# Reordering one DMA queue: from turns of four loads and four stores to turns of three and three

## The chip, the cores and the metric

The kernel runs on one core of one Trainium2 chip. The metric is the device time of one execution in microseconds (us), median over executions. The profile's span, from the first to the last instruction of one profiled execution, is some 1.8 us shorter than the device time of the same execution. TensorE multiplies, VectorE casts, ScalarE copies and SyncE only issues transfers here; PSUM is the memory in which TensorE leaves its products (`ps` in the code). "y of 5" stands for the y of batch 5.

## The reference

```python
def setup_inputs():
    batch, m, k, n = 16, 512, 768, 1024
    return {
        "x": np.random.randn(batch, k, m).astype(np.float32),
        "y": np.random.randn(batch, k, n).astype(np.float32),
    }

def reference(x, y):
    return np.einsum('bkm,bkn->bmn', x, y).astype(np.float32)
```

These are sixteen independent products. Each batch reads 1.57 MB of x and 3.15 MB of y and writes 2.10 MB.

## The kernel before

Every transfer is issued by SyncE, so all go through one DMA queue, in program order. Batch b passes through these stages:

- `load(b)` brings x and y of b into float32 staging tiles (two of each);
- VectorE casts them to bf16 (two of each) and may do so once TensorE has finished batch b-2;
- TensorE multiplies in two groups, each of which fills one half of PSUM;
- ScalarE copies each half into the output buffer `ob[b % 5]`, once store b-5 has landed, and frees the half of PSUM;
- `store(c)` writes batch c out. Its wait is for TensorE to be done with batch c+1, which implies that c has been copied.

```python
    FIRST = 8
    TURN = 4
    NO = 5
    # ... (cut)
    def store(b):
        if b < B - 2:
            nc.sync.wait_ge(groups, 2 * (b + 2))
        else:
            nc.sync.wait_ge(outs, b - (B - 3))
        nc.sync.dma_start(o_v[b], ob[b % NO][:]).then_inc(so[b % NO], 16)

    def load(b):
        i = b % 2
        if b >= 2:
            nc.sync.wait_ge(cast, nx[b - 2])
        wide_dma("x", xs[i][:], x_v[b], 4, True).then_inc(sx[i], 16)
        if b >= 2:
            nc.sync.wait_ge(cast, nx[b - 2] + parts(b - 2))
        wide_dma("y", ys[i][:], y_v[b], 2, True).then_inc(sy[i], 16)

    for b in range(B):
        load(b)
        if b + 1 >= FIRST and (b + 1 - FIRST) % TURN == 0:
            a = b + 1 - FIRST
            for c in range(a, a + TURN):
                store(c)
    for b in range(B - FIRST + TURN, B - 1):
        store(b)

    nc.sync.wait_ge(outs, 2)
    nc.sync.dma_start(o_v[B - 1, :, :HB], ob[(B - 1) % NO][:, :HB]).then_inc(last, 16)
    # ... (cut: casts on VectorE, `ready` on GpSimd)
    with nc.Fori(0, B // 2, engines=pe):
        with nc.Fori(0, 2, engines=pe) as s:
            nc.tensor.wait_ge(ready, 2).then_inc(ready, -2)
            for mo in range(MT):
                g, m = divmod(mo, HB)
                if m == 0:
                    nc.tensor.wait_ge(room, 1).then_inc(room, -1)
                for kt in range(KT):
                    # ... (cut: wait for the second part of y)
                    for nt in range(NT):
                        mm = nc.tensor.matmul(ps[g][:, m, nt], x_w[:, bass.ds(s, 1), kt, mo],
                            yb[:, bass.ds(s, 1), kt, nt * NF:(nt + 1) * NF],
                            start=(kt == 0), stop=(kt == KT - 1))
                if m == HB - 1:
                    mm.then_inc(groups, 1)
    # ... (cut)
    for b in range(B):
        if b >= NO:
            nc.scalar.wait_ge(so[b % NO], 16 * (b // NO))
        for g in range(2):
            nc.scalar.wait_ge(groups, 2 * b + g + 1)
            cp = nc.scalar.copy(ob[b % NO][:, g * HB:(g + 1) * HB].rearrange("p m (t f) -> p m t f", f=NF),
                                ps[g][:])
            if b < B - 1:
                cp.then_inc(room, 1)
            else:
                cp.then_inc(outs, 1)
    # ... (cut)
    for b in range(B - NO, B - 2):
        nc.sync.wait_ge(so[b % NO], 16 * (b // NO + 1))
    section.close()
    nc.sync.dma_start(o_v[B - 1, :, HB:], ob[(B - 1) % NO][:, HB:])
```

Of the kernel before, what the change touches and what calls it, by code (L numbers as in the profile page):

```python
# [3 lines left out]

# [2 lines left out]

# [8 lines left out]
def kernel(  # L16
# [11 lines left out]
    B, K, M = x.shape  # L28
# [9 lines left out]
    y_v = y.rearrange("b (p ko) n -> b p ko n", ko=KT)  # L38
    o_v = out.rearrange("b (p mo) n -> b p mo n", mo=MT)

    FIRST = 8
    TURN = 4
    NO = 5
    KH = KT // 2

# [25 lines left out]
    def wide_dma(key, dst, src, dram_rows, load):  # L71


        if key not in made:
            made[key] = nc.sync.dma_start(dst, src)
            return made[key]
        pat = mybir.BassSymbolicTensorAccessPattern
        widen = lambda a: a.rearrange("(q r) k m -> q (r k m)", r=dram_rows)
        plain = lambda a: a.rearrange("p k m -> p (k m)")
        s, d = (widen(src), plain(dst)) if load else (plain(src), widen(dst))  # L80
        return nc.sync.add_instruction(_copy.replace(
            made[key].ins, name=nc.get_next_instruction_name(),
            ins=(pat(ap=s.ap, dtype=s.dtype, bass_ap=s, is_dma=False),),
            outs=(pat(ap=d.ap, dtype=d.dtype, bass_ap=d, is_dma=False),),
            sync_info=None, ant_dge_precooked=False))


    def parts(b):
        return 2 if b in (15,) else 1
# [2 lines left out]
    nx = [sum(1 + parts(a) for a in range(b)) + 1 for b in range(B)]  # L92



    def store(b):


# [12 lines that stand above are left out]
            nc.sync.wait_ge(cast, nx[b - 2] + parts(b - 2))  # L111
        wide_dma("y", ys[i][:], y_v[b], 2, True).then_inc(sy[i], 16)

    for b in range(B):
        load(b)
        if b + 1 >= FIRST and (b + 1 - FIRST) % TURN == 0:
            a = b + 1 - FIRST
            for c in range(a, a + TURN):
                store(c)
    for b in range(B - FIRST + TURN, B - 1):  # L120
        store(b)


    nc.sync.wait_ge(outs, 2)
# [100 lines left out]
```

## Time and profile before

| | before |
|---|---|
| device time, median of 3 | 260.67 us (260.51 to 260.77) |
| span of the profiled execution | 258.8 us |
| TensorE / VectorE / ScalarE busy | 69% / 32% / 24% |
| DMA queue busy, mean rate | 98.6%, 421 GB/s |
| waits of ScalarE for a store (output buffer) | 3, in total 61.9 us |

In these profiles a line of a timeline reads: start, duration, engine, source line, operation, output from input, shapes, count. The bracket gives how long the engine had been idle before and what ended that. The prediction shows these lines and works from them. The last row of the table is this line of the waits, with the longest wait at its end:

```profile
ACT ob L178 <- DMA out_dram<-ob: 61.9, 3, 21.7
```

### The profile page before, as it was taken

Reading aid. Unit: us, or ns where it says so; the run is one execution under the profiler, and the core shown is the slowest. Engines: PE = TensorE matmul, PEld = TensorE weight load, DVE = VectorE, ACT = ScalarE, POOL = GpSimd, SP = SyncE. Lnnn points to the kernel's source line nnn. Section 1 sums busy time; section 2 is a strip of 40 time slices with the busy share of each in tenths; the row PEclk is TensorE's granted clock in tenths of the full one; section 3 lists DMA queues with packets and bytes.
Section 4 is the critical chain, followed back from the end, with each engine's and each line's share of the span. In section 5 each row is a group of like instructions: output and inputs, shape, how many; then the busy total and the mean of one; then the engine's idle time right before and its main releaser. Section 6 shows DMA issues by size and latency. Waiting matters only on the chain. (4 is left out here: it accounts for less than half of the span.)

```text
span 258.8 us, 2419 instructions
## 1 busy us (share of the span) xinstructions
PE 178.6 (69%) x768; PEld 88.8 (34%) x768; DVE 82.0 (32%) x33; ACT 60.9 (24%) x33; POOL 0.2 (0%) x4
## 2 busy tenths in 40 slices
PE   0019999999999007996599800999579970199950
PEld 0004555555544003553255400455235530045520
DVE  0271644527255250021643624002345272300000
ACT  1000432243220004234022002224302200413430
POOL 0000000000000000000000000000000000000000
PEclk9999999999999756999799975699979995569995
DMA  6999989898999999999999999999899999999996
GB/s 262 444 479 395 486 365 486 365 486 380 471 403 448 377 420 438 453 458 418 433 433 418 441 387 436 420 463 471 380 486 387 463 395 399 436 433 420 441 415 265
DMA packets 4658, 109.07 MB, mean 421 GB/s; under 512 B 784, under 2 KB 784, under 8 KB 784
## 3 DMA queue, kind: packets, MB, share of 16 engines
q1 hardware_dynamic: 4656, 109.06, 98.6%
q14 instruction: 2, 0.02, 0.0%
HBM read 75.50 MB, written 33.55 MB: 421 GB/s over the span
## 5 line engine op out<-in xcount | busy, mean ns | idle before, releaser
L162 PE MATMUL ps<-yb,xb 128*128 x768 | 178.6, 397 | 70.7 <-PEq L157 70.6
L162 PEld LDWEIGHTS ps<-yb,xb 128*128 x768 | 88.8, 116 | 160.0 <-issue 88.5
L178 ACT COPY ob<-ps 128x2048 f32<-128x2048 f32 x32 | 59.6, 1872 | 188.3 <-PE ps L162 126.4
L140 DVE CAST yb<-ys 128x6144 bf16<-128x6144 f32 (+1 forms) x17 | 53.8, 3171 | 80.1 <-DMA ys<-in_y_dram 80.1
L136 DVE CAST xb<-xs 128x3072 bf16<-128x3072 f32 x16 | 28.2, 1760 | 60.0 <-DMA xs<-in_x_dram 48.8
L178 ACT ACT_TABLE_LOAD x1 | 1.3, 1283 | 2.0 <-issue 2.0
L209 POOL MEMSET const-bfloat16-1.0<- 128x1 bf16 x1 | 0.1, 101 | 0.0
L209 POOL MEMSET const-uint8-127<- 128x1 uint8 x1 | 0.1, 101 | 0.0
L209 POOL MEMSET const-float32-0.0<- 128x1 f32 x1 | 0.1, 98 | 0.2 <-issue 0.2
L209 POOL MEMSET const-float32-1.0<- 128x1 f32 x1 | 0.1, 98 | 0.0
## 6 DMA issues: line engine op xcount, KB each, us to landing
ys<-in_y_dram SPq DMA_DIRECT2D x16, 3072.0 KB, 18.6
out_dram<-ob SPq DMA_DIRECT2D x15, 2048.0 KB, 27.4
xs<-in_x_dram SPq DMA_DIRECT2D x16, 1536.0 KB, 20.1
out_dram<-ob SPq DMA_DIRECT2D x2, 1024.0 KB, 7.9
```

Of the source, the lines that this page charges most:

```text
L136: nc.vector.tensor_copy(xb[:, i], xs[i][:]).then_inc(cast, 1)
L140: nc.vector.tensor_copy(yb[:, i, ks], ys[i][:, ks]).then_inc(cast, 1)
L162: mm = nc.tensor.matmul(ps[g][:, m, nt], x_w[:, bass.ds(s, 1), kt, mo], yb[:, bass.ds(s, 1), kt, nt * NF:(nt + 1) * NF], start=(kt == 0), ...
L178: cp = nc.scalar.copy(ob[b % NO][:, g * HB:(g + 1) * HB].rearrange("p m (t f) -> p m t f", f=NF), ps[g][:])
L209: nc = _bacc.Bacc("TRN2", target_bir_lowering=False, num_devices=1)
```

## The change

The intent is shorter turns. ScalarE, and TensorE behind it, should wait less long for an output buffer, and one store's worth less should be left after the last load. Nothing is added or taken away: SyncE issues the same 49 transfers with the same waits, and only their order differs.

```diff
-    FIRST = 8
-    TURN = 4
+    TURNS = [(7, 3), (3, 3), (3, 3), (3, 7)]
     NO = 5
@@
-    for b in range(B):
-        load(b)
-        if b + 1 >= FIRST and (b + 1 - FIRST) % TURN == 0:
-            a = b + 1 - FIRST
-            for c in range(a, a + TURN):
-                store(c)
-    for b in range(B - FIRST + TURN, B - 1):
-        store(b)
+    loads, stores = iter(range(B)), iter(range(B - 1))
+    for nl, ns in TURNS:
+        for b in islice(loads, nl):
+            load(b)
+        for b in islice(stores, ns):
+            store(b)
```

The last store is issued apart in two halves, so "7 stores last" are six whole ones and two halves; before, there were seven whole ones and two halves.

More of the change, by code (lines that the diff above doesn't have):

```diff
@@ L6 @@
 from contextlib import ExitStack
+from itertools import islice
 import concourse.bass as bass
```

## The prediction

> **What bounds the kernel now.** I read the page from the top. Part 1 gives TensorE 69% of the span, VectorE 32% and ScalarE 24%, so no compute engine is full. Parts 2 and 3 show what is full:
>
> ```profile
> DMA  6999989898999999999999999999899999999996
> ...
> q1 hardware_dynamic: 4656, 109.06, 98.6%
> ...
> HBM read 75.50 MB, written 33.55 MB: 421 GB/s over the span
> ...
> PE 9%; ACT 1%; issue 0%
> ```
>
> The first line is the busy share of the 16 DMA engines in 40 slices: 8 or 9 tenths from the second slice to the last but one. The second gives the queue 98.6% of 16 engines' time. The fourth is the chain of waits, and it misleads: it follows only 10% of the span back from the last ScalarE copy, not the transfers that land after that copy. I set it aside and time the queue itself.
>
> For that I use an idle engine as a clock. VectorE casts a tile as soon as its load has landed; where the bracket names the DMA, the start of the cast is the landing time. The timeline of VectorE:
>
> ```profile
> 14.40 3.36 DVE L140 CAST yb<-ys 128x6144 bf16<-128x6144 f32 x1 [5.53 <-DMA ys<-in_y_dram]
> ...
> 80.34 3.36 DVE L140 CAST yb<-ys 128x6144 bf16<-128x6144 f32 x1 [5.46 <-DMA ys<-in_y_dram]
> ...
> 91.51 3.36 DVE L140 CAST yb<-ys 128x6144 bf16<-128x6144 f32 x1 [5.64 <-DMA ys<-in_y_dram]
> 114.76 1.76 DVE L136 CAST xb<-xs 128x3072 bf16<-128x3072 f32 x1 [19.89 <-DMA xs<-in_x_dram]
> 121.99 3.36 DVE L140 CAST yb<-ys 128x6144 bf16<-128x6144 f32 x1 [5.47 <-DMA ys<-in_y_dram]
> ...
> 154.98 3.36 DVE L140 CAST yb<-ys 128x6144 bf16<-128x6144 f32 x1 [5.02 <-DMA ys<-in_y_dram]
> 178.21 1.76 DVE L136 CAST xb<-xs 128x3072 bf16<-128x3072 f32 x1 [19.87 <-DMA xs<-in_x_dram]
> ...
> 218.65 3.43 DVE L140 CAST yb<-ys 128x3072 bf16<-128x3072 f32 x2 [4.92 <-DMA ys<-in_y_dram]
> ```
>
> These are the landings of y for batches 0, 6 and 7, x and y for 8, y for 11, x for 12 and y for 15.
> - **A load** (x and y of one batch, 4.72 MB): (80.34 - 14.40)/6 = 10.99 us, or 429 GB/s. In this stretch the casts came on time and nothing was stored.
> - **A store** (2.10 MB): from y of 7 to x of 8, 23.25 us pass (23.23 in the second turn). The x load is a third of a load, 3.66 us; four stores take the other 19.58, so 4.89 each, or 428 GB/s. That includes one change from loads to stores and one back.
>
> So both directions run at one rate, and the two changes of direction together cost 4 x 4.89 less 4 x (2.10 MB at 429 GB/s = 4.88), under 0.1 us.
>
> **The end** in the timelines of ScalarE and SyncE:
>
> ```profile
> 223.51 3.63 ACT L178 COPY ob<-ps 128x2048 f32<-128x2048 f32 x2 [20.02 <-DMA out_dram<-ob]
> ...
> 249.32 1.86 ACT L178 COPY ob<-ps 128x2048 f32<-128x2048 f32 x1 [2.95 <-PE ps L162]
> ```
>
> ```profile
> 246.40 0.33 SPq L125 DMA_DIRECT2D out_dram<-ob  x1
> 251.38 0.33 SPq L194 DMA_DIRECT2D out_dram<-ob  x1
> ```
>
> After y of 15 landed at 218.65, eight stores' worth of bytes remain: 218.65 + 8 x 4.88 = 257.69. The last half store, issued at 251.38, took 6.7 us to land (shortest time to landing of that tile), so 258.08. The queue therefore ran without a gap to the end; the half store's turn came at about 257.69 - 2.44 = 255.25, 3.9 us after its issue. The compute tail is hidden behind stores, with a margin of 3.9 us.
>
> **What the Trainium skill says.** "DMA: Bandwidth & Descriptors", section "Where 436 GB/s comes from", puts the ceiling of the 16 ports at 435 GB/s; 429 here is within 2% of it, so a better order has no rate left to win. Its section "Two DMAs through the same engine are not ordered" says that descriptors of one queue start in order but are pipelined; the changes of direction under 0.1 us agree. "TensorE: Matmul & The Clock Gate", section "What's actually happening", says that an idle array falls to half clock after a window of about 3.4 us; the trace agrees (granted clock 0.50 from 90 to 100 us, 1.00 from 105), but TensorE isn't the bound.
>
> **The change, part by part.** The order of instructions on PE, VectorE, ScalarE and GpSimd is the same. SyncE issues the same 49 transfers with the same sizes and waits, in another order. Before: 8 loads, 4 stores, 4 loads, 4 stores, 4 loads, 7 stores and two halves. After: 7, 3, 3, 3, 3, 3, 3, then 6 stores and two halves.
> 1. Bytes: 16 x 10.99 + 16 x 4.88 = 253.9 us of queue in both. Change: 0.
> 2. Changes of direction: 5 before, 7 after. The start: y of 0 landed at 14.40, one load of 10.99 earlier is 3.41. Before, 3.41 + 253.9 = 257.3, against a last landing at 258.08; so five changes and every other gap together cost 0.8 us, at most 0.16 each. Two more: 0 to +0.3, and I take +0.1.
> 3. Waits for staging and output buffers, which could leave the queue empty. Loads: y of batch b is issued after the cast of y of b-2, some 3.4 us after that landed, when all of batch b-1 (11 us) is still in front of it; the same rule, and the same margin of 7 us, hold in both orders. The cast also needs TensorE to be done with b-2, and TensorE may wait for an output buffer. There are five; the copy of batch b waits for store b-5. After the change, y of 6 lands at 80.3, stores 0 to 2 run to 95.0 and y of 7, 8, 9 land at about 106.0, 117.0, 127.9. Store 0 lands at 85.2 and releases the copy of batch 5; TensorE starts batch 6 some 2.2 us later (before: 223.51 to 225.74), at 87.4, and ends it at 98.6 with 48 matmuls in about 11.2. The cast of x of 8 (landing at 110) and store 5 (in turn at 137) are the next things that need it. Margins are over 10 us. The turn repeats every 3 x (10.99 + 4.88) = 47.6 us, so it does at 7-9, 10-12 and 13-15. Change: 0.
> 4. The tail: y of 15 lands at about 223.5, 4.9 us later, with seven stores' worth behind it, 34.2 us. Store 9 is first and lands at 228.4; TensorE starts batch 15 at 230.6 and ends near 243 (before, two batches took 23.54 from a cold start, so about 12.3 for one), and the last copy ends near 245 instead of 251.18. The last half store gets its turn at 255.3, so the margin grows from 3.9 to about 10 us. It was hidden before, so this gains 0.
>
> Sum: +0.1 us on 260.67, **260.8 us**.
>
> **The rivals.**
> - *The tail or the queue was in fact not full, and the larger margin gains something.* For: the middle stretch 143.98 to 154.98 shows 401 GB/s and the last 410. Against: landings in those same stretches are 11.00 us for a load, and 39.43 us for eight stores, so the dip is the way that long packets are counted. All that could be won is the 0.8 us of item 2: 260.0.
> - *More changes of direction cost.* If a change drained the pipeline, two more would cost by as much as the drain. Against: under 0.1 us for two of them. Even 0.5 us each makes 261.7.
> - *A new wait on SyncE.* It issues in order, so a store that waits for TensorE blocks the loads behind it. If my margin of 10 us were wrong in each of three turns by some 5 us more, +15: 275. In the profile before, the longest wait for TensorE (26.6 us at a store) left the queue full; nothing speaks for it.
> - *A warmer TensorE.* Its long gaps (14.8, 13.9 and 13.8 us) become shorter ones. It would change TensorE's busy time by a few us and the end by nothing.
>
> **Range and chances.** Executions before spread from 260.51 to 260.77. The second rival's modest form reaches 261.5, the first 260.0. So 260.8, with 260.1 to 261.5 for 8 times in 10. Being over 2% (5.2 us) faster is impossible for a full queue with the same bytes, short of a rate above anything seen: 0.01. Over 2% slower needs the third rival: 0.02. Within 2%: 0.97.
>
> **What would show it.** The queue's share stays at 98 to 99%, 420 to 422 GB/s. Landings of y stay 11.0 us apart inside a turn; from y of 6 to x of 7 pass 3 x 4.88 + 3.66 = 18.3 us, three times over. ScalarE waits for stores four times by about 10 us (10.5 at the first: its copy ends at 74.7, store 0 lands at 85.2), 41 us in place of the three waits that sum to 61.9. TensorE's long gaps are three of about 11 us, with four of about 4. The last copy ends near 245. If a load's landing comes more than 12 us after the one before inside a turn, the queue ran dry and item 3 is wrong; if the 18.3 comes out as 18.6 or more, item 2 is; if y of 15 to the end takes under 34 us, the tail had held something back.

## The result, and the profile after

The changed kernel takes 260.83 us (median of 4, 260.68 to 261.35), the kernel before 260.59 in the executions beside it. The ratios in this document are worked out from fast runs of the same rounds, so they are not quite the ratios of the medians. Here it is 1.0011, with a 95% interval of 0.9996 to 1.0026: the same.

The queue and the bytes, in the page of the changed kernel:

```profile
DMA  6999989999999999999999999989999899999995
...
q1 hardware_dynamic: 4656, 109.06, 98.5%
```

It is as full as before. The landings, in VectorE's timeline of the changed kernel (y of 5 and 6, x of 7; y of 9, x of 10; y of 12, x of 13; y of 15):

```profile
69.42 3.36 DVE L137 CAST yb<-ys 128x6144 bf16<-128x6144 f32 x1 [4.74 <-DMA ys<-in_y_dram]
...
80.73 3.36 DVE L137 CAST yb<-ys 128x6144 bf16<-128x6144 f32 x1 [5.68 <-DMA ys<-in_y_dram]
99.09 1.76 DVE L133 CAST xb<-xs 128x3072 bf16<-128x3072 f32 x1 [15.01 <-DMA xs<-in_x_dram]
...
128.33 3.36 DVE L137 CAST yb<-ys 128x6144 bf16<-128x6144 f32 x1 [4.42 <-DMA ys<-in_y_dram]
146.66 1.76 DVE L133 CAST xb<-xs 128x3072 bf16<-128x3072 f32 x1 [14.97 <-DMA xs<-in_x_dram]
...
175.88 3.36 DVE L137 CAST yb<-ys 128x6144 bf16<-128x6144 f32 x1 [4.30 <-DMA ys<-in_y_dram]
194.59 1.76 DVE L133 CAST xb<-xs 128x3072 bf16<-128x3072 f32 x1 [15.35 <-DMA xs<-in_x_dram]
...
223.79 3.43 DVE L137 CAST yb<-ys 128x3072 bf16<-128x3072 f32 x2 [4.36 <-DMA ys<-in_y_dram]
```

Three stores and an x take 18.36, 18.33 and 18.71 us. The one load that came late is y of 6, 11.31 us after y of 5 instead of 10.99. The last y lands 5.1 us later than before, because one store more now runs ahead of it.

What moved lies beside the queue. The waits of ScalarE, and its timeline at the end, in the changed kernel:

```profile
ACT ob L175 <- DMA out_dram<-ob: 38.1, 4, 10.5
```

```profile
228.81 3.64 ACT L175 COPY ob<-ps 128x2048 f32<-128x2048 f32 x2 [9.27 <-DMA out_dram<-ob]
236.76 1.87 ACT L175 COPY ob<-ps 128x2048 f32<-128x2048 f32 x1 [4.32 <-PE ps L159]
241.58 1.87 ACT L175 COPY ob<-ps 128x2048 f32<-128x2048 f32 x1 [2.94 <-PE ps L159]
```

There are four waits of at most 10.5 us in place of three of about 21, so 24 us less in total. The last copy ends at 243.45 instead of 251.18. None of this reaches the end, because the queue is still writing stores then: the last half store lands at 258.39 (issued at 249.19, 9.2 us to landing), against 258.08 before. Its line in SyncE's timeline:

```profile
249.19 0.33 SPq L191 DMA_DIRECT2D out_dram<-ob  x1
```

### The profile page after: what moved, and what is told of

Same layout as the page of the kernel before. It is cut to its first block, busy times and chain, and to the rows that moved or that the text cites. A ratio compares the mean times of both kernels' runs of the same rounds, so it can differ in the third digit from the quotient of the medians.

```text
span 259.1 us, 2419 instructions
## 1 busy us (share of the span) xinstructions
PE 176.2 (68%) x768; PEld 88.3 (34%) x768; DVE 82.0 (32%) x33; ACT 60.8 (23%) x33; POOL 0.2 (0%) x4
## 3 DMA queue, kind: packets, MB, share of 16 engines
q1 hardware_dynamic: 4656, 109.06, 98.5%
## 5 line engine op out<-in xcount | busy, mean ns | idle before, releaser
L159 PE MATMUL ps<-yb,xb 128*128 x768 | 176.2, 393 | 65.4 <-PEq L154 65.3
```

## The experiments

Theory A is that the queue is always full, so the time is its bytes over one rate. The order is then free, as long as no store or load comes up for its turn before it is ready. Rival B: each change of direction costs something that other savings hid. Rival C: mixing directions changes the rate. Rival D: parts of the change move the time by more than 1 us each and cancel. The table below gives each experiment with its time and that of the kernel before in the same rounds. A landing is called late against 10.99 us for each load and 4.88 for each store, counted from y of batch 0. The four e_tail runs were made on another chip than the other runs in the table; each is compared with the kernel before in its own rounds.

| run | order (loads, stores) | us | before, us | ratio (95%) |
|---|---|---|---|---|
| e_single | 7,1, then 8 times 1,1, then 1,7 | 261.08 | 260.67 | 1.0018 (1.0005 to 1.0032) |
| e_first8 | 8,3, 3,3, 3,3, 2,7 | 260.34 | 260.67 | 0.9995 (0.9981 to 1.0008) |
| e_turn4 | 7,4, 4,4, 5,8 | 260.94 | 260.67 | 1.0011 (0.9997 to 1.0025) |
| e_long | 10,8, 6,8 | 268.82 | 260.67 | 1.0319 (1.0303 to 1.0335) |
| e_tail3 | 5,3, 3,3, 3,3, 3,3, 1,1, 1,3 | 266.44 | 260.83 | 1.0220 (1.0203 to 1.0237) |
| e_tail4 | 5,3, 3,3, 3,3, 3,3, 2,4 | 264.45 | 260.83 | 1.0137 (1.0118 to 1.0156) |
| e_tail5 | 5,3, 3,3, 3,3, 3,2, 2,5 | 261.94 | 260.83 | 1.0044 (1.0027 to 1.0060) |
| e_tail9 | 9,4, 4,3, 3,9 | 263.52 | 260.83 | 1.0100 (1.0083 to 1.0117) |
| e_halfbytes | as changed, six stores halved | 246.05 | 260.70 | 0.9441 (0.9427 to 0.9455) |
| e_pe_after | as changed, TensorE +1/3 | 261.47 | 260.70 | 1.0033 (1.0017 to 1.0048) |
| e_pe_before | as before, TensorE +1/3 | 266.90 | 260.70 | 1.0253 (1.0223 to 1.0283) |
| e_two_queues | no turns, stores on ScalarE's queue | 262.96 | 260.70 | 1.0090 (1.0075 to 1.0105) |

All gave correct results except e_halfbytes, which leaves outputs unwritten.

### Is it the bytes?

```diff
-        nc.sync.dma_start(o_v[b], ob[b % NO][:]).then_inc(so[b % NO], 16)
+        h = HB if 3 <= b < 9 else MT
+        nc.sync.dma_start(o_v[b, :, :h], ob[b % NO][:, :h]).then_inc(so[b % NO], 16)
```

> The changed kernel, with the stores of batches 3 to 8 cut to their first half (a wrong result on purpose: half of those rows are never written). No wait is taken away. Theory A (the time is the bytes of the one queue over its rate): six halves of 2.44 us less, -14.6 us against the changed kernel, 246.2 (range 245 to 247.5), the queue's share still 98%. Rival (something beside the bytes sets the pace in the middle, TensorE or a buffer): less than 10 us gained, and the queue's share falls.

Measured: 246.05 us. Against the kernel before in the same rounds that is 14.65 us less; the changed kernel was 0.24 above it in its own rounds. In the page of this run the queue is as full as ever:

```profile
q1 hardware_dynamic: 4656, 102.76, 98.6%
```

Six half stores of 2.44 us make 14.6. The middle of the kernel is paced by bytes; nothing else shows, at least down to this size of turn.

### Do the parts of the change cancel?

The edits are the list of turns alone:

```diff
-    TURNS = [(7, 3), (3, 3), (3, 3), (3, 7)]
+    TURNS = [(8, 3), (3, 3), (3, 3), (2, 7)]     # e_first8
+    TURNS = [(7, 4), (4, 4), (5, 8)]             # e_turn4
```

> 8 loads first as before, then turns of three, 7 stores last: the changed kernel with one load more at first. Theory A: within 0.4 us of both kernels, 7 changes of direction. Rival (the first loads and the turns each move the time by more than 1 us and cancelled): this one lies 1 us or more off.

> 7 loads first as in the changed kernel, turns of four, 8 stores' worth last as before, 5 changes of direction. Theory A: within 0.4 us of both kernels. Rival (parts that cancel): 1 us or more off, to the other side than e_first8.

Measured: 260.34 and 260.94, both within 0.4 us of the kernel before, with intervals that include 1. Rival D is out: neither the step from 7 to 8 first loads nor that from turns of three to turns of four moves the time by 1 us. e_first8 has the lowest median of all orders, but it can't be told from the kernel before.

### What does a change of direction cost?

```diff
-    TURNS = [(7, 3), (3, 3), (3, 3), (3, 7)]
+    TURNS = [(7, 1)] + [(1, 1)] * 8 + [(1, 7)]   # e_single: 19 changes of direction
+    TURNS = [(10, 8), (6, 8)]                    # e_long: 3 changes
```

> Turns of one load and one store, 7 loads first and 7 stores last as in the changed kernel: 19 changes of direction in place of 7 (5 in the kernel before). Theory A (the queue is full and a change of direction costs under 0.16 us): +0.6 us over the kernel before, at most +2.3. Rival B (a change drains the pipeline, 0.5 us or more, and other savings of the new order hid it in the first result): +7 us or more. Rival C (mixing the two directions is good for the rate): faster by 1 us or more. Queue share 98% or more under A.

> 10 loads, 8 stores, 6 loads, then the rest: only 3 changes of direction, the fewest. Theory A says the order is free only while no store waits for TensorE with an empty queue; here it does. Reckoned from the rows of the two profiles: y of 9 lands at 113.3 us, store 0 at 118.2, TensorE starts batch 6 at 120.4 and ends 6, 7, 8 at 132.6, 143.2, 153.8. Store 6 needs 7 and has its turn at 142.6, store 7 needs 8 and has its turn at about 150: gaps of some 2.6 and 5.7 us, so +8 us over the kernel before, 268.7 (range +5 to +11). Rival (fewer changes of direction are what counts): the same time or faster.

Measured for e_single: 261.08, so 0.41 us over the kernel before with 14 changes more, or 0.03 us each by the medians. Its profiled execution was the slowest of the six (262.29 us, span 260.5), so it shows more of the loss than the median has, and how the loss comes. It is not the same at every change. VectorE's timeline of e_single, x of 8 and 9 at the start and y of 14, x and y of 15 at the end:

```profile
105.40 1.76 DVE L133 CAST xb<-xs 128x3072 bf16<-128x3072 f32 x1 [5.24 <-DMA xs<-in_x_dram]
...
121.36 1.76 DVE L133 CAST xb<-xs 128x3072 bf16<-128x3072 f32 x1 [5.36 <-DMA xs<-in_x_dram]
...
208.63 3.36 DVE L137 CAST yb<-ys 128x6144 bf16<-128x6144 f32 x1 [5.69 <-DMA ys<-in_y_dram]
217.63 1.76 DVE L133 CAST xb<-xs 128x3072 bf16<-128x3072 f32 x1 [5.64 <-DMA xs<-in_x_dram]
225.17 3.43 DVE L137 CAST yb<-ys 128x3072 bf16<-128x3072 f32 x2 [5.78 <-DMA ys<-in_y_dram]
```

One load and one store should take 10.99 + 4.88 = 15.87 us. From x of 8 to x of 9 it was 15.96; the last turn, y to y, took 16.54. Over the kernel y of 15 was 2.0 us late in this execution (0.56 in the changed kernel, 0.36 before). Rival B, at 0.5 us a change, is out. Rival C, that mixing gains, is out as well. Why some turns cost nothing and others 0.2 to 0.7 us is not settled, but they are not scattered: the late ones are the last four of the nine turns. Turns of three part the same way. In the changed kernel, e_tail3, e_tail4 and e_tail5 the first two turns (three stores and an x) took 18.27 to 18.53 us and every later one 18.69 to 18.82. It is not the hour, as the second turn of the kernel before ran beside the third of e_tail3 in time (from 154.98 and 154.23) and lost nothing. So the loss sits in late turns for a reason that stays open, and that a change of direction as such costs anything is not shown.

e_long has the fewest changes and is 8.1 us slower, where 8 were reckoned. DMA's row of its page, and its timelines of SyncE, then of VectorE:

```profile
DMA  7999899899899899899994399989989989999997
```

```profile
95.78 59.12 SPq L102 DMA_DIRECT2D out_dram<-ob  x8
154.94 0.48 SPq L75 DMA_DIRECT2D xs<-in_x_dram  x1
```

```profile
165.63 1.76 DVE L133 CAST xb<-xs 128x3072 bf16<-128x3072 f32 x1 [16.39 <-DMA xs<-in_x_dram]
```

The 4 and the 3 are the hole. SyncE spent 59 us on eight stores, because the last ones waited for TensorE, which had waited for the first store to free an output buffer. The loads behind them in program order could not be issued. x of 10, above, and y of 10 (172.87) land 9.0 us late, and that delay stays. This is the third rival of the prediction. It is real, and it showed with eight stores in a turn and five output buffers; turns of three and four are free of it, and lengths between were not tried.

### How short, and how long, may the tail be?

```diff
+    TURNS = [(5, 3), (3, 3), (3, 3), (3, 3), (1, 1), (1, 3)]   # e_tail3
+    TURNS = [(5, 3), (3, 3), (3, 3), (3, 3), (2, 4)]           # e_tail4
+    TURNS = [(5, 3), (3, 3), (3, 3), (3, 2), (2, 5)]           # e_tail5
+    TURNS = [(9, 4), (4, 3), (3, 9)]                           # e_tail9
```

> Five loads first, turns of three and one, and 3 stores' worth of bytes after the last load (14.6 us of queue). Theory A: the time is the queue's as long as the last copy is done and its store issued (about 2 us ahead) before its turn. Here batch 15 isn't held up by an output buffer: its cast ends 3.4 us after the last load, 48 matmuls take about 11, the copy 1.9, the issue 2: 19 us after the landing, against a turn at 12.2. So the end is exposed by about 7 us: 267.6 (range +5 to +9). Rival (the end is always hidden, whatever is left): 260.6 to 261.

> The same with 4 stores' worth after the last load (19.5 us of queue, turn of the last half at 17.1, ready at 19): exposed by about 2 us, 262.6 (range +1 to +4).

> The same with 5 stores' worth after the last load (turn of the last half at 22.0, ready at 19): hidden, the time of the kernel before within 0.6 us.

> Nine loads first, turns of four and three, and 9 stores' worth after the last load (43.9 us of queue). Now the five output buffers hold TensorE up: the copy of batch 12 waits for store 7, first in the tail, so batches 13, 14 and 15 start 7 us after the last landing, take 23.5 + 11, the copy 1.9, the issue 2: ready at 45.7 against a turn at 41.5: exposed by about 4 us, 264.8 (range +2 to +6). Rival (more stores at last are always safe): 260.6 to 261.

Measured over the kernel before: +5.6, +3.6, +1.1 and +2.7 us. The shape is as expected: exposed at 3 and 4, free from 5, exposed again at 9. All ranges but e_tail5's hold, and three sizes were reckoned badly.

For e_tail3, 7 us were reckoned, and the range held partly by luck. In its profile y of 15 landed at 244.56 and the last half store was issued at 259.71, 15.2 us later instead of 19: TensorE started 2.3 us after the landing and took 10.73, and the store was issued 0.2 us after the last copy instead of 2. From y of 15 to the end (259.71 + 3.9) passed 19.05 us for 14.64 of stores, so the tail itself exposed 4.4. The rest is that y of 15 was 1.3 us late, and y of 0 landed at 14.95 instead of 14.40.

For e_tail4, the timelines of VectorE, then SyncE:

```profile
239.41 3.43 DVE L137 CAST yb<-ys 128x3072 bf16<-128x3072 f32 x2 [5.27 <-DMA ys<-in_y_dram]
```

```profile
257.77 0.33 SPq L191 DMA_DIRECT2D out_dram<-ob  x1
```

The last half store was issued 18.4 us after the last landing and took 4.3 to land. Of that 2.44 is data, so I estimate its data 1.9 us behind its issue: ready at 20.3 against a turn at 17.1, so 3.2 us exposed instead of 2. Here too y of 15 was 1.3 us late. TensorE had started batches 14 and 15 after 14 us of idling and did the 96 matmuls in 23.52 us instead of 21.1 (twice the 10.55 of a batch at full clock). In e_tail5 the tail itself is hidden: y of 15 at 234.15, the end at 252.10 + 6.9 = 259.0, that is 24.85 us for 24.4 of stores. Its 1.1 us are lost elsewhere, and I can place only part: y of 15 is late by 0.71 us instead of 0.36, and y of 0 landed at 14.91 instead of 14.40. That last has nothing to do with the order, as the same two loads are issued first in both, and e_long and e_pe_before had it too (14.93 each); the kernels before of those rounds have no profile to compare, so it stays open.

In e_tail9 TensorE did the last three batches in 33.40 us from 221.14 and the last half store was issued at 256.63. That is 42.3 us after the last load's landing, reckoned at 214.3 (its cast waited for TensorE, so no clock shows it). With 1.9 us to its data it was ready at 44.2, 2.7 after its turn at 41.5; I had reckoned 45.7.

### How much slack does TensorE have?

```diff
-                    for nt in range(NT):
-                        mm = nc.tensor.matmul(...
-                            start=(kt == 0), stop=(kt == KT - 1))
+                    for r in range(3 if kt == 0 else 1):
+                        for nt in range(NT):
+                            mm = nc.tensor.matmul(...
+                                start=(kt == 0), stop=(kt == KT - 1 or (kt == 0 and r < 2)))
```

> The changed kernel with the first of six steps of each group of matmuls done three times (each starts afresh, so the result is right): a third more TensorE work, about 14.3 us a batch in place of 10.7. Theory A with a margin of some 10 us at the end: batch 14 ends about 10 us after the last load, batch 15 about 14.4 later, copy 1.9 and issue 1.9: ready at 28 of a turn at 31.7: hidden, within 1 us of the changed kernel.

> The same third more TensorE work in the kernel before. There batches 14 and 15 both start only after store 8 has released an output buffer, 7.1 us after the last load, and take 23.5 x 4/3 = 31.4; with copy and issue ready at 42.3 against a turn at 36.6: exposed by about 5.7 us, 266.4 (range +4 to +8). If both this and e_pe_after keep the time, the margins of 3.9 and 10 us that I read from the profiles are wrong.

Measured: 261.47 and 266.90 us with the same added work. By spans, 259.6 and 264.5, so +0.5 and +5.7 over the kernels that they were made from. The issues of the last half store, in e_pe_before and then e_pe_after:

```profile
259.81 0.33 SPq L195 DMA_DIRECT2D out_dram<-ob  x1
```

```profile
250.96 0.33 SPq L192 DMA_DIRECT2D out_dram<-ob  x1
```

This is what the change is worth, though the time doesn't show it. In the order before, batches 14 and 15 both wait for the first store of the tail; in the new order only batch 15 does (TensorE's last starts: 96 matmuls at 225.74 before, 48 at 231.00 after). With a TensorE a third slower, the new order is 5.4 us faster than the old one (266.90 - 261.47).

### Both directions in flight at once

```diff
-        for b in islice(stores, ns):
-            store(b)
@@ ScalarE, after its copies of batch b
+        if b >= 1:
+            nc.scalar.dma_start(o_v[b - 1], ob[(b - 1) % NO][:]).then_inc(so[(b - 1) % NO], 16)
@@
-    for b in range(B - NO, B - 2):
+    for b in range(B - NO, B - 1):
```

> No turns: loads alone on SyncE's queue, each store issued by ScalarE on its own queue as soon as the next batch is done, so that both directions are in flight together. Theory A (the rate is the same whatever the mix, and what the order does is to leave stores for the time after the last load): by the last load 13 of 16 stores are done, so it lands at 3.4 + 175.8 + 63.4 = 242.7, and batch 15, its copies and its stores follow with a nearly empty queue: +26 us, with the end 269.5 (range +5 to +12 over the kernel before). Rival (in flight together both directions go faster than 430 GB/s): the last load lands clearly before 242, and the time may fall below 260.

Measured: 262.96 us, +2.3 where I expected +5 to +12 (the "+26 us" in the text counts from the last load). The rate, in a table by stage (VectorE's columns and others between; the last number is GB/s), and the last y:

```profile
49.62:217.71 168.09, 128.97 (x535) 62.37 (x534) 56.32 (x22) 41.08 (x22) 0.00 (x0) 0.90 1.00 432
```

```profile
233.03 3.43 DVE L135 CAST yb<-ys 128x3072 bf16<-128x3072 f32 x2 [8.16 <-DMA ys<-in_y_dram]
```

The mixed rate is 432 GB/s by this view, which gives 429 for loads alone, so mixing is worth under 1%. The last load landed at 233.0, not 242.7. My term "13 of 16 stores done by then" was wrong. At 429 GB/s, the 229.5 us from the start of the first load make 98.5 MB, of which 75.5 are loads: 11 stores are done. The two queues don't share evenly. Landings of y come 15.17 us apart, which at 429 GB/s is 6.51 MB: 4.72 of a load and 1.79 of stores, less than the 2.10 that each batch makes, so stores fell behind and were left for the tail by themselves. One likely reason was not tested, the size of packets. The queues of this run's page, SyncE's (loads and two half stores) and then ScalarE's (15 stores):

```profile
q1 hardware_dynamic: 2496, 77.60, 69.5%
q10 hardware_dynamic: 2160, 31.46, 28.2%
```

The mean packet is 31.1 KB on the first and 14.6 KB on the second, so equal numbers of packets would already be 2.1 to 1 in bytes; 4.72 to 1.79 is 2.6 to 1.

The tail then lost some to a wait of my own making: SyncE waited for stores 11 to 14 to land (7.0 us at the longest) and issued the last half at 256.50, when its data was done at 249.6.

## Why the prediction was right

1. **Bytes** (change 0): held. e_halfbytes shows it directly, with 14.65 us for a reckoned 14.6.
2. **Changes of direction** (+0.1, 0 to +0.3): held in sum, but not tested in size, as 0.1 is within the noise. All that lies beyond the first load's start and the reckoned queue was 0.8 us before; after, 258.39 - (14.46 - 10.99) - 253.9 = 1.0. The picture of an even cost did not hold: one of the three turns took 18.71 us, over the 18.6 that I had named as a sign against this step, the other two 18.36 and 18.33. e_single shows the same: small on average, uneven, with the loss in the late turns. The prediction's "under 0.1 us" for two changes also rested on an assumption: it took 4.88 for a store from the rate of loads. Turns of two lengths give it without that. The first five turns of e_single took 15.89 us on average (y of 6 at 80.83 to y of 11 at 160.28), 4.90 beyond a load; the turns of four took 19.58 beyond an x. The three stores between make 4.89 each, which leaves some 0.0 us for two changes, so the reading stands.
3. **Buffers** (0): held. ScalarE's four waits sum to 38.1 us for a reckoned 41, the longest 10.5 as reckoned. TensorE's gaps were 10.2, 11.9 and 12.1 us for three of about 11, and 4.0, 2.9, 2.9 and 3.0 for four of about 4. e_long shows that the wait which I had ruled out does exist once a turn is too long.
4. **The tail** (0): held. The last copy ended at 243.45 instead of near 245, because I took batch 15 to start at half clock (12.3 us); after a gap of only 3.00 us it took 10.55, at full clock, where batch 6 after a gap of 3.98 us took 12.24. The window of about 3.4 us that the prediction quotes from the Trainium skill lies between the two, but other runs here show that the length of the gap alone does not decide. In e_two_queues a batch after 2.31 us took 12.11 (granted clock 0.50 at its start), and one after 3.52 us took 10.55. So the full clock at the end could not have been reckoned from the gap. TensorE's timelines, of the changed kernel and then of e_two_queues:

```profile
87.83 12.24 PE L159 MATMUL ps<-yb,xb 128*128 x48 [3.98 <-PEq L154]
...
231.00 10.55 PE L159 MATMUL ps<-yb,xb 128*128 x48 [3.00 <-PEq L154]
```

```profile
175.48 12.11 PE L157 MATMUL ps<-yb,xb 128*128 x48 [2.31 <-PEq L152]
...
221.64 10.55 PE L157 MATMUL ps<-yb,xb 128*128 x48 [3.52 <-PEq L152]
```

That the larger margin is real, and buys nothing while TensorE is fast enough, is shown by the pair with a third more TensorE work. From y of 15 to the end passed 34.6 us, not under 34, so nothing had been held back there. I had put the margin at the end of the copies; the last half store is really issued after a further wait for an earlier store, at 249.19, still 6.8 us before its turn at about 255.9.

So a rearrangement that cut 24 us of one engine's waits moved the time by 0.24 us, within noise: those waits were never what the queue waited for.

## What to carry to other kernels

Before reordering transfers on a full queue, add up bytes over the measured rate, from the start of the first load: if that sum reaches the last landing to within 1 us (here 0.8), a better order can win no more than that, and a worse one can lose (8.1 us in e_long). The order still has a window: a tail after the last load long enough to hide the last batch (five stores here) and turns short enough that no store waits for a compute engine that waits for a store. When two orders take the same time, the one with more slack at the end is worth keeping; slow the hidden engine on purpose to show that slack.

## What the Trainium skill lacked or had wrong

- "DMA: Bandwidth & Descriptors", section "Where 436 GB/s comes from", says that the HBM side, about 358 GB/s, binds transfers between HBM and SBUF. For one core alone it did not bind: 429 GB/s loading and 428 storing here. The "HBM Reference" page, section "Specifications (TRN2)", has it right for a core that streams alone (about 425).
- No page has the rate of stores from SBUF to HBM on trn2 (428 GB/s here; the one table of stores is for trn3), or what changing direction inside one queue costs: here 0.03 us each over 14 more changes by the medians of e_single, where the loss sits in the last four turns of nine.
- "DMA: Bandwidth & Descriptors", section "Queues, rings and completion order", has two queues served in turn by packets, but not what share of the bytes follows: here 4.72 MB of loads to 1.79 MB of stores, though stores were behind, with mean packets of 31.1 and 14.6 KB.
- "TensorE: Matmul & The Clock Gate", section "What's actually happening", has half clock follow an idle window of about 3.4 us. Here it followed gaps of 2.31 us (e_two_queues) and 2.66 us (e_single).
